# A two-layer diffusion trunk: the order of the projections, the place of the spatial gating, and pooling on GpSimd

## The chip, the cores and the metric

The kernel runs on one core of a Trainium2 chip. The metric is the device time of the whole program in microseconds (us), the median of several runs of it. Five engines work side by side, each through its own instructions in order: PE (TensorE, matmuls and transposes), DVE (VectorE), ACT (ScalarE), POOL (GpSimd) and SP (SyncE, which here only issues loads). They wait for each other on semaphores.

## The reference

A trunk of two layers on 512 latent tokens and 256 context tokens of width 1024. In each layer a modulated layer norm feeds one projection, whose columns go to four mixers; their outputs are joined, projected, and followed by a squared-ReLU network. Layer 1 keeps only what the latent tokens need: of the context it takes keys and values. Cut to the mixers:

```python
z = h @ w_in[l]                       # hc: the same for context tokens
k, v, kn, kr, vm = kv_sources(z[..., C_KV:], mla_kv_norm[l], mla_w_ukv[l])
k = apply_axial_rope(k, swa_ang_h)
q = apply_axial_rope(cols(z, C_SWA_Q, W_SWA_Q).reshape(...), swa_ang_h)
qn, qr = mla_expand_q(cols(z, C_MLA_CQ, W_MLA_CQ), mla_q_norm[l], mla_w_uq[l])
y = jnp.concatenate([
    pool_mixer(...),    # means over windows of 2, 4, 8, 16 tokens, minus the token
    swa_latent(...),    # softmax over a band of 3 blocks, the context and a sink
    mla_latent(...),    # softmax over all latent and context tokens
    sgu_mixer(...),     # u * (w_s @ layer_norm_affine(v) + b_s), with u, v = gelu(z)
], axis=-1) @ w_out[l]
```

## The kernel before, in words

Everything is float32. A matmul is made of three on parts: each operand is split into a high part (rounded by ACT) and a low part (the difference, by DVE), and high x high, high x low and low x high are added up in PSUM. So each loaded weight, and each result that goes into another matmul, passes through ACT and then DVE. The splits of loaded weights are L162 (ACT) and L165 (DVE); those of results are L145 and L146 or, with a factor, L149 and L150.

The function `mixers` computes a layer's four mixers. Its projections are called by the columns of the weight that they take:

- wb, by token: the latent queries before their norm (cq, kept in tiles cqL for latent and cqC for context tokens) and the gate's v (vgL, vgC). Its eviction `ev_b` ends with a multiply and an add by the gate norm's constants sgb (L632, L633).
- wp, by feature: the pooling mixer's input, in two tiles of features, f 0 (windows 2 and 4) and f 1 (8 and 16). Its eviction, in `pool`, copies it into a padded tile xp and makes the means by additions of shifted copies in pa and pb, and writes the difference pd.
- wk: the windowed keys. `ev_k` copies them to kf, rotates kf (a shuffle L437 and a multiply L438 on DVE, a multiply L439 on POOL, an add L440 on DVE) and splits them into kh (ACT) and kl (DVE, L654).
- wq: the windowed queries, two tiles, the same way (qf, then qs, L676).
- wu: the gate's other half u, with a gelu on ACT (L696).
- wa, by token, three groups of two token tiles: the values v, the latent keys and values before their norm (ckv) and the rotary key.

Then come the spatial gating `sgu` (a transposed weight wsT, matmuls mix, on DVE an add of bs and a multiply by u into mx, and a split into yh and yl), transposes of cq (cqT) and of ckv (ckT, krT) with their splits, and vm, the latent values. After that comes attention, in units of one query block for a pair of heads: `scores(x)`, softmax, `turn(x-1)` (the transposes pT), `values(x-2)` (the matmuls o). A table `todo` hangs other work on a unit: `rotary` (uqr, and the splits of rt and krl) on unit 1, the steps of the later heads' queries and keys on others; between them `fill` puts the ada matmuls, which make the next modulation from a streamed weight wada. In this loop the order is fixed as it is written (`self.pin`). Outside it a scheduler orders each engine's instructions by dependencies and a timeline that it plans at build; weight loads on SP's queue keep the order in which they are written.

Buffers are pools: PSUM has tiles of one bank (A, three; F, one) and of two banks (S, two, which the projections and the scores share); in SBUF the tag T, six tiles, holds xp, rc, pa, pb, kf, qf, the gate's ws, wsT and mx, p's transposes and more. A tile is handed on when its last reader is done.

## Time and profile before

| what | us |
|---|---|
| median of 3 runs (1570.26 to 1573.25) | 1571.64 |
| the profiled execution | 1570.16 |
| its span on the core | 1568.4 |
| PE busy in it | 1481.3 |
| DVE busy | 922.7 |
| ACT busy | 565.7 |
| POOL busy | 222.0 |

The profiled execution's time lies 1.8 us above its span, and 1.48 below the median of the runs. Busy times are sums over the span; they say which engine has room, not which one the end waits for. For that there is the chain that ended last, which is followed back from the last instruction. Matmuls are pipelined, so PE counts as busy also where its pace is lower; PEclk is the clock that PE was granted, as a share of the full one.

### The profile page before, as it was taken

The page shows a single profiled execution, that of the slowest core. Times are in us where ns is not written, and L with a number is a line of the kernel's source. Part 1 is how long each engine was busy: PE and PEld are TensorE (multiplying, and loading weights), DVE is VectorE, ACT ScalarE, POOL GpSimd, SP SyncE. Part 2 cuts the span into 40 slices and gives each one's busy share as a digit, 9 for nine tenths or more (in the row PEclk, how much of TensorE's full clock was granted, in tenths as well). Part 3 has the DMA queues.
Part 4 walks back from the last instruction along what each step waited for, and adds up shares of the span by engine and source line. Part 5 has one row for each costly group of instructions (what it writes and reads, how often), then busy time and mean ns, then how long its engine had stood idle before and what let it go on. Part 6 is the DMA issues. An engine that isn't in the chain of part 4 may idle for free.

```text
span 1568.4 us, 23456 instructions
## 1 busy us (share of the span) xinstructions
PE 1481.3 (94%) x9438; PEld 1246.7 (79%) x9438; DVE 922.7 (59%) x1615; ACT 565.7 (36%) x1000; POOL 222.0 (14%) x244
## 2 busy tenths in 40 slices
PE   5899889999999999999999989989998999999996
PEld 3689677787988888888888868867776888888885
DVE  4385755547545445454454798675645656655557
ACT  4433555524621221312113156355625433222322
POOL 1021334223000000000000062143222000000003
PEclk9999999999999999999999999999998999999998
DMA  8441366362232121211211223235363433333221
GB/s 296 152 120 55 112 219 195 108 242 89 81 108 65 49 76 54 76 59 55 81 55 67 81 94 111 64 109 178 120 208 108 147 95 95 95 101 92 88 81 54
DMA packets 148069, 169.93 MB, mean 108 GB/s; under 512 B 8776, under 2 KB 96248, under 8 KB 147960
## 3 DMA queue, kind: packets, MB, share of 16 engines
q1 hardware_dynamic: 137912, 149.94, 30.7%
q10 hardware_dynamic: 10048, 18.49, 3.5%
q8 instruction: 74, 1.21, 0.3%
q14 instruction: 35, 0.29, 0.1%
HBM read 164.19 MB, written 4.22 MB: 107 GB/s over the span
## 4 chain that ended last, share of the span: by engine, by line
PE 84%; DVE 7%; DMA 3%; ACT 2%; issue 1%; POOL 1%; SPq 0%; ACTq 0%; POOLq 0%; DVEq 0%
PE ff L133 54%; PE wo L133 5%; PE wb L133 3%; PE o L133 3%; PE pT L188 2%; PE wa L133 2%; PE ada L133 2%; PE wp L133 2%; PE wu L133 2%; PE wq L133 2%; PE sm L133 2%; DMA wada<-in_w_ada 1%; DVE nmax L533 1%; PE wk L133 1%; PE hT L188 1%
## 5 line engine op out<-in xcount | busy, mean ns | idle before, releaser
L162 ACT ACTIVATE hiw<-raww 128x1024 fp32r<-128x1024 f32 x120 | 126.8, 1062 | 565.8 <-PE ff L133 565.8
L165 DVE TENSOR_TENSOR low<-raww,hiw 128x1024 fp32r<-128x1024 f32 x120 | 146.3, 1223 | 245.3 <-ACT hiw L162 245.3
L133 PE MATMUL ff<-low,fh 128*128 128x512 f32 x640 | 249.0, 389 | 0.0
L133 PE MATMUL ff<-hiw,fl 128*128 128x512 f32 x640 | 249.0, 389 | 0.0
L133 PE MATMUL ff<-hiw,fh 128*128 128x512 f32 x640 | 247.9, 389 | 0.0
L133 PE MATMUL ff<-hl,hiw 128*128 128x512 f32 (+1 forms) x672 | 237.9, 354 | 0.0
L133 PE MATMUL ff<-hh,hiw 128*128 128x512 f32 (+1 forms) x672 | 237.8, 354 | 0.0
L133 PE MATMUL ff<-hh,low 128*128 128x512 f32 (+1 forms) x672 | 237.7, 354 | 0.0
L1274 DVE TENSOR_TENSOR fft<-ff,gate 128x512 f32<-128x512 f32 x160 | 110.0, 687 | 100.2 <-PE ff L133 100.2
L133 PEld LDWEIGHTS ff<-hh,hiw 128*128 128x128 f32 x672 | 127.1, 189 | 17.9
L133 PEld LDWEIGHTS ff<-hl,hiw 128*128 128x128 f32 x672 | 127.1, 189 | 17.7
L133 PEld LDWEIGHTS ff<-hh,low 128*128 128x128 f32 x672 | 127.0, 189 | 17.7
L133 PEld LDWEIGHTS ff<-hiw,fl 128*128 128x128 f32 x640 | 120.1, 188 | 25.0
L133 PEld LDWEIGHTS ff<-hiw,fh 128*128 128x128 f32 x640 | 120.2, 188 | 24.8
L133 PEld LDWEIGHTS ff<-low,fh 128*128 128x128 f32 x640 | 120.1, 188 | 24.7
L1275 POOL TENSOR_TENSOR x<-x,fft 128x512 f32<-128x512 f32 x14 | 20.3, 1452 | 837.5 <-DVE fft L1274 832.5
L547 POOL TENSOR_SCALAR p<-p,rec 128x768 f32<-128x768 f32 (+3 forms) x80 | 63.1, 793 | 142.0 <-DVE rec L546 132.1
L1275 DVE TENSOR_TENSOR x<-x,fft 128x512 f32<-128x512 f32 x114 | 78.7, 690 | 2.9
L133 PE MATMUL ada<-wada,sc 128*32 128x128 f32 x1536 | 60.7, 295 | 20.0 <-DMA wada<-in_w_ada 20.0
L133 PEld LDWEIGHTS ada<-wada,sc 128*32 128x32 f32 x1536 | 41.8, 116 | 34.1 <-DMA wada<-in_w_ada 13.1
L188 PE MATMUL pT<-ident,p 128*128 128x128 f32 x368 | 55.9, 279 | 9.9 <-ACT pT L555 4.4
L133 PE MATMUL wo<-lowo,yh 128*128 128x512 f32 x160 | 62.5, 390 | 0.5 <-DVE lowo L165 0.5
(335 smaller groups left out, 2749.7 us busy)
## 6 DMA issues: line engine op xcount, KB each, us to landing
raww<-in_w_ff SPq DMA_DIRECT2D x120, 512.0 KB, 4.2
wada<-in_w_ada SPq DMA_DIRECT2D x96, 512.0 KB, 4.6
rawwo<-in_w_out SPq DMA_DIRECT2D x16, 512.0 KB, 6.1
rawz<-in_w_ff SPq DMA_DIRECT2D x8, 512.0 KB, 5.6
rawwb<-in_w_in SPq DMA_DIRECT2D x12, 256.0 KB, 4.1
gate<-grow ACTq DMA_DIRECT2D x6, 512.0 KB, 6.8
badab<-in_b_ada SPq DMA_DIRECT2D x36, 64.0 KB, 3.9
x<-in_x SPq DMA_DIRECT2D x4, 512.0 KB, 4.4
```

The costliest lines, as they stand in the source:

```text
L133: return self.pinned(self.nc.tensor.matmul(out, lhsT, rhs, start=start, stop=stop))
L162: i = nc.scalar.activation(out=hi, in_=raw, func=AF.Copy)
L165: nc.vector.tensor_tensor(out=lo, in0=raw, in1=hi.bitcast(F32), op=ALU.subtract)
L188: return self.pinned(self.nc.tensor.transpose(out, in_, self.ident if ident is None else ident))
L533: nc.vector.tensor_reduce(out=nm, in_=S[:, lo:hi], axis=AX.X, op=ALU.max, negate=True)
L547: nc.gpsimd.tensor_scalar(out=p[:, :keep], in0=p[:, :keep], scalar1=rec, scalar2=1.0, op0=ALU.mult, op1=ALU.mult)
L1274: nc.vector.tensor_tensor(out=t, in0=ps, in1=g[:, sl], op=ALU.mult)
L1275: eng.tensor_tensor(out=xt[:, sl], in0=xt[:, sl], in1=t, op=ALU.add)
```

## The change

Five edits, which change the place and the engine of work, and none of what is computed:

1. In `ev_b`, the multiply and the add by sgb move from DVE to POOL: six token tiles in layer 0, four in layer 1, two operations of 128x256 each.
2. The transposes and splits of cq (cqT) move from behind `sgu` to right behind wb.
3. The projection wu moves from ahead of wa to behind vm, so the keys' and values' steps stand between wa and wu in the program; its weights are loaded after wa's.
4. `sgu` is called on unit 2 of the attention loop, no longer ahead of it, and its multiply by u moves from DVE to POOL.
5. In `pool`, the memsets of xp move to POOL, and so do the means of f 0; those of f 1 stay on DVE.

```diff
--- before.py
+++ after.py
@@ -629,8 +629,8 @@
             )
             m, r = self.stats(lambda _: v, 1)
             nc.vector.tensor_scalar(out=v, in0=v, scalar1=m, scalar2=r, op0=ALU.subtract, op1=ALU.mult)
-            nc.vector.tensor_tensor(out=v, in0=v, in1=P["sgb"][:, 0, :], op=ALU.mult)
-            nc.vector.tensor_tensor(out=v, in0=v, in1=P["sgb"][:, 1, :], op=ALU.add)
+            nc.gpsimd.tensor_tensor(out=v, in0=v, in1=P["sgb"][:, 0, :], op=ALU.mult)
+            nc.gpsimd.tensor_tensor(out=v, in0=v, in1=P["sgb"][:, 1, :], op=ALU.add)
 
         gb = list(zip(preps, gr))
         self.proj_tok(l, gb if full else gb[:2], [(512, 768), (1024, 1280)], 2, ev_b, "wb", self.wb_first,
@@ -639,6 +639,15 @@
         if not full:
             preps[2]()
 
+
+        cqT = [(self.Z("cqh"), self.Z("cql")) for _ in range(2)]
+        for k in range(2):
+            for s, nt, c0 in ((0, LT, 0), (1, CT, NL)) if full else ((0, LT, 0),):
+                pt = self.PA("cqT")
+                for i in range(nt):
+                    self.tr(pt[:, 128 * i:128 * i + 128], CQ[s][:, i, 128 * k:128 * k + 128])
+                n = 128 * nt
+                self.split(cqT[k][0][:, c0:c0 + n], cqT[k][1][:, c0:c0 + n], pt[:, :n], P["gq"][:, k:k + 1])
 
         pool_finish = self.pool(l, P, hL, hC, yL, yC, full)
 
@@ -688,16 +697,6 @@
                     q_split(pc, 2 * f + j, NL, NL + NC, 0.125)
 
         self.proj_T(l, hL, hC, 256, 2, ev_q, full, "wq")
-
-
-        U = [self.Z("u", F32) for _ in range(2)]
-
-        def ev_u(f, pl, pc):
-            nc.scalar.activation(out=U[f][:, :NL], in_=pl, func=AF.Gelu)
-            if full:
-                nc.scalar.activation(out=U[f][:, NL:], in_=pc, func=AF.Gelu)
-
-        self.proj_T(l, hL, hC, 768, 2, ev_u, full, "wu")
 
 
         V = self.X([128, 6, 128], "v")
@@ -736,18 +735,6 @@
 
         Wq = load_heads(A["mla_w_uq"][l].rearrange("(k p) n -> p k n", p=128), 64, 96, "uq")
         Wk = load_heads(A["mla_w_ukv"][l].rearrange("(k p) n -> p k n", p=128), 64, 128, "ukv")
-
-        self.sgu(l, P, U, VG, yL, yC, full)
-
-
-        cqT = [(self.Z("cqh"), self.Z("cql")) for _ in range(2)]
-        for k in range(2):
-            for s, nt, c0 in ((0, LT, 0), (1, CT, NL)) if full else ((0, LT, 0),):
-                pt = self.PA("cqT")
-                for i in range(nt):
-                    self.tr(pt[:, 128 * i:128 * i + 128], CQ[s][:, i, 128 * k:128 * k + 128])
-                n = 128 * nt
-                self.split(cqT[k][0][:, c0:c0 + n], cqT[k][1][:, c0:c0 + n], pt[:, :n], P["gq"][:, k:k + 1])
         ckT = (self.Z("ckh"), self.Z("ckl"))
         krf = self.T("krf", 768)
         for i0, nt, c0 in ((0, LT, 0), (LT, CT, NL)):
@@ -773,6 +760,16 @@
                 nc.vector.tensor_copy(out=dst, in_=pv[:, 0:256])
             else:
                 nc.scalar.activation(out=dst, in_=pv[:, 0:256], func=AF.Copy)
+
+
+        U = [self.Z("u", F32) for _ in range(2)]
+
+        def ev_u(f, pl, pc):
+            nc.scalar.activation(out=U[f][:, :NL], in_=pl, func=AF.Gelu)
+            if full:
+                nc.scalar.activation(out=U[f][:, NL:], in_=pc, func=AF.Gelu)
+
+        self.proj_T(l, hL, hC, 768, 2, ev_u, full, "wu")
 
 
         nq = NL + NC if full else NL
@@ -919,7 +916,7 @@
                 out_pair(O[0], NC if stream else NL, 2 + part, stream)
 
 
-        todo = {1: [rotary]}
+        todo = {1: [rotary], 2: [lambda: self.sgu(l, P, U, VG, yL, yC, full)]}
 
         def plan(part, x0, x1):
             t = part - 2
@@ -985,13 +982,13 @@
                 if ps is None:
                     continue
                 xp = self.pt.tile([128, NL + 16], F32, name=self.nm("xp"), tag="T")
-                nc.vector.memset(xp[:, 0:8], 0.0)
-                nc.vector.memset(xp[:, 8 + n:16 + n], 0.0)
+                nc.gpsimd.memset(xp[:, 0:8], 0.0)
+                nc.gpsimd.memset(xp[:, 8 + n:16 + n], 0.0)
                 x = xp[:, 8:8 + n]
                 nc.scalar.activation(out=x, in_=ps, func=AF.Copy)
                 rc = self.T("rc")
                 nc.scalar.dma_start(out=rc[:, :n], in_=A["rcnt"][f, :, c0:c0 + n])
-                tt = nc.vector.tensor_tensor
+                tt = (nc.vector if f else nc.gpsimd).tensor_tensor
                 a = self.pt.tile([128, NL + 16], F32, name=self.nm("pa"), tag="T")
                 b = self.pt.tile([128, NL + 16], F32, name=self.nm("pb"), tag="T")
                 e = 8 + n
@@ -1056,7 +1053,7 @@
                     in0=ps[:, :n].rearrange("p (c q) -> p c q", q=128),
                     in1=P["bs"][:, f, :].unsqueeze(1).to_broadcast([128, nt, 128]), op=ALU.add,
                 )
-                nc.vector.tensor_tensor(out=t[:, :n], in0=t[:, :n], in1=U[f][:, c0:c0 + n], op=ALU.mult)
+                nc.gpsimd.tensor_tensor(out=t[:, :n], in0=t[:, :n], in1=U[f][:, c0:c0 + n], op=ALU.mult)
                 if stream == 0:
                     y = (self.HL("yh"), self.HL("yl"))
                     yL[6 + f] = y
```

How the edits move instructions is seen in the order of each engine. In the rows below a row is line, operation, output<-inputs and size; x8 stands for eight alike. Rows of before have its line numbers, rows of after its own.

On PE, the end of wa in layer 0; s are the scores of unit 0. Before:

```order
L133 MATMUL wa_1540<-lowa_1403,hh_337 128x288
L133 MATMUL wa_1540<-hiwa_1402,hl_338 128x288
L188 MATMUL wsT_1625<-ident,ws_1623 128x128 x4
L133 MATMUL s_1778<-maskR,identR 128x256
L133 MATMUL s_1778<-kh_1042,qs_1124 128x256
L133 MATMUL s_1778<-kl_1044,qs_1124 128x256
L133 MATMUL s_1778<-kh_1042,qs_1124 128x256
L133 MATMUL s_1778<-kl_1044,qs_1124 128x256
L133 MATMUL mix_1632<-wsT_1630,vgL_341 64x128 x8
```

After:

```order
L133 MATMUL wa_1451<-lowa_1314,hh_337 128x288
L133 MATMUL wa_1451<-hiwa_1313,hl_338 128x288
L188 MATMUL ckT_1537<-ident,ckv_1298 128x128 x3
L188 MATMUL krT_1544<-ident,ckv_1298 96x128 x3
L133 MATMUL wu_1598<-hh_307,hiwu_1603 128x512
L133 MATMUL wu_1598<-hl_308,hiwu_1603 128x512
L133 MATMUL wu_1598<-hh_307,lowu_1604 128x512
L133 MATMUL wu_1598<-hh_309,hiwu_1603 128x512
```

The gating (wsT, mix) is gone from here, the transposes of ckv are the next thing after wa, and wu's matmuls follow.

On POOL in layer 0's projections, ahead of kf's rotation (L439); rsq and brs are roots for the norms. Before:

```order
L173 TENSOR_TENSOR rsq_832<-rv_835,mhalf 128x1
L173 TENSOR_TENSOR brs_843<-rv_844,mhalf 128x1
L173 TENSOR_TENSOR rsq_851<-rv_854,mhalf 128x1
L173 TENSOR_TENSOR brs_862<-rv_863,mhalf 128x1
L439 TENSOR_TENSOR kf_1101<-kf_1101,swa_t_869 128x512
L439 TENSOR_TENSOR qf_1239<-qf_1239,swa_t_869 128x512
```

After:

```order
L633 TENSOR_TENSOR vgC_342<-vgC_342,sgb_649 128x256
L1008 TENSOR_TENSOR pd_901<-pb_1021,xp_1014 128x512
L996 TENSOR_TENSOR pa_1033<-xp_1027 128x258
L997 TENSOR_TENSOR pb_1034<-pa_1033,rc_1031 64x256
L998 TENSOR_TENSOR pb_1034<-pa_1033 64x256
L985 MEMSET xp_1040 128x8
L986 MEMSET xp_1040 128x8
L999 TENSOR_TENSOR pb_1034<-pb_1034,rc_1031 64x256
L1008 TENSOR_TENSOR pd_901<-pb_1034,xp_1027 128x256
L985 MEMSET xp_1055 128x8
L986 MEMSET xp_1055 128x8
L439 TENSOR_TENSOR kf_1129<-kf_1129,swa_t_869 128x512
```

Gate operations (L632, L633) and the means of f 0 (L996 to L999, L1008) now stand ahead of kf's multiply.

On DVE, around unit 2 of layer 0's attention; nmax is the softmax's maximum, rec its reciprocal. Before:

```order
L591 COPY pT_1965<-pT_1972 128x128
L146 TENSOR_TENSOR rt_1921<-rt_1898,rt_1920 128x768
L146 TENSOR_TENSOR krl_1925<-krf_1718,krh_1924 32x768
L863 COPY s_2012<-sink_647 128x1
L546 RECIPROCAL rec_1961<-den_1959 128x1
L533 TENSOR_REDUCE nmax_2019<-s_2012 128x1
L863 COPY s_2027<-sink_647 128x1
L533 TENSOR_REDUCE nmax_2034<-s_2027 128x1
```

After:

```order
L591 COPY pT_1900<-pT_1907 128x128
L146 TENSOR_TENSOR rt_1856<-rt_1833,rt_1855 128x768
L146 TENSOR_TENSOR krl_1860<-krf_1536,krh_1859 32x768
L546 RECIPROCAL rec_1896<-den_1894 128x1
L1037 COPY wsT_1948<-wsT_1943 128x512
L1051 TENSOR_TENSOR mx_1959<-mix_1950,bs_652 128x512
L1051 TENSOR_TENSOR mx_1975<-mix_1966,bs_652 128x512
L146 TENSOR_TENSOR yl_1963<-mx_1959,yh_1962 128x512
L1051 TENSOR_TENSOR mx_1987<-mix_1982,bs_652 128x256
L1051 TENSOR_TENSOR mx_1999<-mix_1994,bs_652 128x256
L146 TENSOR_TENSOR yl_1979<-mx_1975,yh_1978 128x512
L860 COPY s_2012<-sink_647 128x1
```

The copy of wsT (L1037), the four adds of bs (L1051) and the splits yl (L146) stand behind krl, ahead of the next maxima.

## Rows read from the trace of the kernel before

**Rows 1.** The page's chain that ended last, over the whole span, by engine.

```profile
PE 84%; DVE 7%; DMA 3%; ACT 2%; issue 1%; POOL 1%; SPq 0%; ACTq 0%; POOLq 0%; DVEq 0%
```

**Rows 2.** The chain of layer 0's projections: start us, us, what.

```profile
107.18 16.72 PE wq L133 x96
123.90 16.70 PE wu L133 x96
...
161.86 1.28 ACT L542
...
169.03 0.66 DVE cql L150
...
186.34 0.66 PE pT L188 x6
```

**Rows 3.** Busy time by stretches: us, then busy per engine (x), PEclk, DMA share, GB/s.

```profile
96.00:140.00 44.00, 44.00 (x261) 39.14 (x260) 38.66 (x72) 18.30 (x32) 5.01 (x4) 1.00 0.31 87
159.50:186.34 26.84, 22.39 (x228) 18.27 (x227) 20.50 (x52) 13.60 (x32) 7.08 (x8) 0.94 0.36 108
172.00:175.50 3.50, 1.25 (x8) 0.79 (x8) 3.47 (x8) 2.61 (x6) 0.66 (x2) 1.00 0.57 190
175.50:179.50 4.00, 3.25 (x12) 2.69 (x12) 3.02 (x10) 0.77 (x2) 1.81 (x3) 0.57 0.03 2
957.00:993.00 36.00, 34.39 (x168) 28.13 (x166) 34.93 (x75) 19.44 (x38) 6.82 (x7) 1.00 0.40 110
1023.40:1045.36 21.96, 19.26 (x202) 15.32 (x201) 17.54 (x42) 11.65 (x27) 6.52 (x8) 1.00 0.35 120
```

**Rows 4.** PE's waits, 945 to 1024: waited for, us in total, times, longest.

```profile
PE wu L133 <- DVE kl L654: 1.2, 1, 1.2
```

**Rows 5.** The chain of layer 1's projections.

```profile
993.38 11.14 PE wu L133 x48
```

**Rows 6.** PE's timeline behind wa, layer 0: start us, us, engine line op.

```profile
179.97 0.28 PE L133 MATMUL vm<-hiukv,ckl 128*128 128x256 f32 x1
180.09 0.28 PE L133 MATMUL vm<-hiukv,ckh 128*128 128x256 f32 x1
```

**Rows 7.** DVE's timeline in layer 0, two windows; [idle before, releaser].

```profile
88.06 1.09 DVE L632 TENSOR_TENSOR vgL<-vgL,sgb 128x256 f32<-128x256 f32 x3 [2.30 <-DMA sgb<-in_sgu_norm_g]
...
109.07 0.69 DVE L1008 TENSOR_TENSOR pb<-pa 64x512 f32<-64x512 f32 x1
...
114.61 1.43 DVE L1008 TENSOR_TENSOR pb<-pa 64x256 f32<-64x256 f32 x1
...
116.79 0.42 DVE L1009 TENSOR_TENSOR pb<-pb,rc 64x256 f32<-64x256 f32 x1
...
122.83 0.87 DVE L654 TENSOR_TENSOR kl<-wk,kh 64x256 fp32r<-64x256 f32 x2
...
190.45 1.44 DVE L146 TENSOR_TENSOR krl<-krf,krh 32x768 fp32r<-32x768 f32 x1
```

**Rows 8.** POOL's timeline, layer 0's projections.

```profile
90.67 0.54 POOL L173 TENSOR_TENSOR rsq<-rv,mhalf 128x1 f32<-128x1 f32 x1 [6.57 <-DVE rv L172]
...
114.38 1.36 POOL L439 TENSOR_TENSOR kf<-kf,swa_t 128x512 f32<-128x512 f32 x1 [16.65 <-DVE rsh L437]
```

**Rows 9.** POOL's groups, whole span, by form: busy us, mean ns, idle before.

```profile
L1275 POOL TENSOR_TENSOR x<-x,fft 128x512 f32<-128x512 f32 x14 | 20.3, 1452 | 837.5 <-DVE fft L1274 832.5 <-DVE sm L347 2.5 <-DVE rv L172 2.5
...
L547 POOL TENSOR_SCALAR p<-p,rec 128x256 f32<-128x256 f32 x16 | 7.5, 478 | 19.4 <-DVE rec L546 19.1
```

**Rows 10.** ACT's timeline, layer 0's projections.

```profile
112.93 0.60 ACT L661 ACTIVATE kf<-wk 128x512 f32<-128x512 f32 x1 [4.30 <-DVE pd L1011]
```

**Rows 11.** The waits of SP's DMA queue, 150 to 330.

```profile
SPq L116 <- PE ada L133: 82.3, 23, 8.9
```

**Rows 12.** The chain in layer 0's attention.

```profile
232.68 4.35 DMA wada<-in_w_ada
...
275.00 5.21 DMA rawwo<-in_w_out
```

## The prediction, made before the changed kernel ran

> **What bounds the kernel now.** I read the page's chain first: PE holds 84% of the chain that ended last, DVE 7% [rows 1]. So what can be won is PE's idle time in the stages that the change touches, not work of the other engines. I then read the chain around the projections of both layers, the table by stretches, and the timelines of the engines behind the places where the chain leaves PE.
>
> In layer 0 PE runs wq and wu back to back, 107.18 to 140.6 [rows 2], then wa; in the stretch 96 to 140 it has no idle at all, although DVE is busy 38.66 of 44.00 us there [rows 3]. After wa the chain breaks up into pieces of other engines until the pT at 186.34 that feeds the first o [rows 2]: PE is busy 22.39 of these 26.84 us, DVE 20.50 [rows 3]. The stall is the preparation of keys, values and spatial gating, which go through DVE and ACT in turn. In the worst of it, 172 to 175.5, PE is busy 1.25 of 3.50 us, and the stretch behind that ran at a granted clock of 0.57, mostly the lower level, 1.2 of 2.4 GHz [rows 3]. Layer 1 repeats it: PE 19.26 of 21.96 us [rows 3]; there the wu before it also waits 1.2 us for DVE's kl [rows 4], in a stretch in which DVE is busy 34.93 of 36.00 [rows 3].
>
> **The change, part by part.** All sums are against the profiled execution's own time, 1570.16 us; the median of the three runs is 1571.64, that is 1.48 more, and the sum is carried over to it.
>
> *wu behind the keys and values.* wu is moved, not removed: 16.70 us in layer 0, 11.14 in layer 1 [rows 2, 5]. What stood between wa and the first o can now run under wu's matmuls. Counted from start to start in PE's timeline, at the pace of the full clock (vm 0.12 us each [rows 6]), PE's own work between 159.50 and 186.34 is about 19.0 us: wsT 0.45, mix 2.7, cqT 1.3, ckT and krT 1.6, vm 18 x 0.12 = 2.1, uqr 2.2, scores 4.8, pT 0.9, ada 2.9. Of it 4.5 (wsT, mix, cqT) leaves for another place, 14.5 stays. The rest, 26.84 - 19.0 = 7.8, is waiting and lower clock. I leave 1.0 of waiting in, because ACT has to load a table (1.28 us [rows 2]) between wu's gelu and the next exp. So the window shrinks by 26.84 - 14.5 - 1.0 = **11.3** in layer 0, by 12.3 at most. In layer 1 the same count gives 17.0 of 21.96, of which 3.1 leaves and 13.9 stays; with 0.7 of waiting left it shrinks by **7.4**, by 8.1 at most.
>
> *cqT under the projections.* 12 transposes in layer 0, 1.3 us of PE; 8 in layer 1, 0.9; and their splits on DVE, 0.66 for 512 columns [rows 2], about 2.1 in all in layer 0, in a stretch where DVE is nearly full. PE's share is in the next term.
>
> *What wu covered before.* This is the cost. In layer 0 wu starts at 123.90 [rows 2] and DVE's last kl ends at 123.70 [rows 7]: the keys are split just in time, and then wu's 16.7 us cover the queries' split. Now wa stands there. It needs the PSUM tile that wk gives back with kl, and for its third group one that is given back on DVE behind all of the qs. Two things move kl. DVE loses the pooling means of f 0 (512 columns 5 x 0.69, 256 columns 5 x 0.42 [rows 7]), two splits of wu's weights and most of the gate's operations; it gains cqT's. But kf's rotation is POOL's L439 (1.36 [rows 8]), which now stands behind 12 gate operations and 10 pooling operations on POOL's queue, and f 1's pooling on DVE needs tiles of a pool that POOL holds longer. POOL's two-tensor operation on 512 columns took 1.45 us; on 256 columns the trace has none, and I bound it by 0.48, the one-tensor operation of that width, and 0.75, half of the 512 [rows 9]. From 88.06, when the gate's constants have landed [rows 7]: 12 x 0.48 to 0.75, 5 x 1.45, 5 x 0.48 to 0.75, 6 root operations of 0.54 [rows 8], which ends between 107 and 111.5 if POOL never waits. kf came off PSUM at 112.93, after ACT had waited 4.30 for a pooling tile [rows 10]. POOL does wait, for xp from 97 on, so that wait for a tile grows rather than shrinks. The start of wa shifts against the old start of wu by 1.3 (cqT alone) to 7; I take **+4**, nearest to the row of a tile that waits. In layer 1 there is no context to pool, POOL has five such operations, and DVE sheds 8 x 0.42 + 5 x 0.69 + two weight splits (2.4) and gains 1.3 of cqT: 7.8 us less ahead of kl. The wait of 1.2 goes, 0.9 of cqT comes: **-0.3** (to +3).
>
> Two rows speak against this part: DVE's L1008 on 64x256 took 1.43 us at 114.61, inside POOL's L439, where an operation of the same size took 0.42 two microseconds later [rows 7, 8]. The Trainium skill ("SBUF — State Buffer", section "SBUF: two separate sides") has a rule that agrees: the two engines share a port pair as an exclusive lock, held for a whole instruction, against DVE operations with two SBUF inputs. By the rule moved work costs DVE part of what it saves, and the sum becomes the second rival's.
>
> *Spatial gating inside attention.* wsT and mix remain PE work: **+3.1** in layer 0, **+2.2** in layer 1. At unit 2 mix waits for DVE's copy of wsT, which stands behind nmax, pT copies, rt's and krl's L146 (krl 1.44 [rows 7]); PE's next pT stands behind mix; and the four multiplies on POOL stand ahead of later units' p. Followed in order, with every piece at its duration, PE loses 4.4 us in layer 0, at the least 1 if waits that are there anyway take the rest; I take **+3**, and **+2** (0 to 3) in layer 1.
>
> *Weight loads.* SP's loads of wada wait for PE's ada matmuls, 82.3 us in the stretch [rows 11], so they move with PE: no cost, but see the third rival.
>
> Sum: layer 0, 4 - 11.3 + 3.1 + 3 = -1.2; layer 1, -0.3 - 7.4 + 2.2 + 2 = -3.5. Together -4.7: 1565.5 for the profiled run, **1567.0** for the median. All terms at their bounds: layer 0 -6.9 to +3.2, layer 1 -6.2 to +0.8, so 1558.5 to 1575.6.
>
> **The rivals.** *Full gain.* Every cover holds: 1.3 - 12.3 + 3.1 + 1 and -0.3 - 8.1 + 2.2 + 0, together -13.1, so 1558.5. For it: DVE sheds over 7 us in each stretch where it is nearly full. Against: at unit 2 DVE's order is fixed, and wsT's copy is behind the two longest operations there.
>
> *Slower: GpSimd and DVE in each other's way.* Before kl in layer 0, DVE has some 20 operations with two SBUF inputs; one that met a POOL operation lost 1.0 us (1.43 - 0.42). If seven meet one, kl is 7 later on top of the 4, and in layer 1, if the same uses up what DVE sheds, the shift is +3 in place of -0.3. That is -4.7 + 7 + 3.3 = +5.6: 1577. It decides from 4.7 of such losses on. For it: DVE is 88 to 97% busy in both stretches. Against: POOL has 22 and 13 operations, and only those that run beside the chain to kl count.
>
> *The time is given back.* In layer 0's attention PE waits 4.35 us for wada at 232.68 and 5.21 for rawwo at 275.00 [rows 12]. If those land when they did, what layer 0 gains is waited away there, and layer 1's -3.5 shrinks to within noise with a late unit 2: -4.7 + 1.2 + 2 = -1.5, so 1570. Against it: their issue follows PE.
>
> **How the numbers follow.** About 0.2% (3.1 us) is what a measurement of this kernel can tell from no change. Forecast, -3.1 to -9: 0.42. Full gain, beyond -9: 0.12. Given back, or terms that cancel, within 3.1: 0.26. Slower: 0.20. So faster 0.54, same 0.26, slower 0.20. The range goes from the full gain, 1558.5, to the slower rival's price, 1577, and leaves about one in ten out on either side.
>
> **What would show it.** In the changed profile: from wa's end to the first o no long piece of DVE in the chain and a granted clock of 1 (window step); wa's start against 123.9 and the end of the last kl (cover step); in layer 1 no wait for kl; a wait of mix for wsT's copy, 1 to 4 us (unit-2 step); pooling operations of 1.4 us on DVE where POOL runs (lock); waits for wada and rawwo no longer than before. The prediction is wrong if wa starts after 132 in layer 0, if unit 2 costs over 5 us, or if landings hold attention where it was.

## The result, and the profile after

The changed kernel took 1581.47 us (median of four runs, 1581.25 to 1586.07); the kernel before, on the same chip, 1570.95 (four runs, 1569.59 to 1573.25). The ratio is 1.0072, with a 95% interval of 1.005 to 1.0095: slower by 0.7%. The prediction was 1567.0, in a range from 1558.5 to 1577: faster was forecast, the kernel is slower, and its time lies above the range. The profiled execution took 1581.32 us at a span of 1579.5; before it was 1570.16 at 1568.4, so 11.1 us of span are to be explained.

The page's chain of the changed kernel, by engine, against [rows 1]:

```profile
PE 78%; DVE 8%; DMA 4%; POOL 4%; ACT 3%; issue 2%; SPq 0%; ACTq 0%; POOLq 0%; DVEq 0%
```

PE gave up 6 points of the chain to everything else; POOL, which had 1%, has 4%. The table by stretches (columns as in [rows 3]) says where that is and where it isn't:

```profile
96.00:130.00 34.00, 29.84 (x194) 27.14 (x193) 24.18 (x41) 12.56 (x23) 18.83 (x24) 1.00 0.27 77
150.70:181.80 31.10, 31.10 (x260) 27.60 (x258) 14.75 (x36) 14.54 (x31) 6.96 (x8) 1.00 0.40 123
182.00:188.35 6.35, 1.94 (x49) 1.53 (x47) 5.13 (x10) 3.51 (x7) 2.94 (x3) 0.99 0.56 186
188.35:197.00 8.65, 6.30 (x52) 5.36 (x53) 4.01 (x6) 1.26 (x2) 2.54 (x2) 0.62 0.04 15
1025.10:1049.80 24.70, 24.70 (x208) 21.12 (x206) 14.59 (x36) 11.17 (x26) 6.98 (x8) 1.00 0.47 149
```

The second and the last row are the stretch from wa's end to the first o, with wu in it: PE has no idle time and the full clock, in both layers. The first row is layer 0's projections, which had no idle time before: now PE idles 4.2 of 34.0 us, and DVE, which was nearly full, is busy 24.18: it waits too. The third and fourth rows are the attention's units 1 and 2, where spatial gating now stands: PE is busy 1.94 of 6.35 us, and then comes a stretch at a granted clock of 0.62.

PE's waits from 100 to 1200 us, the stretch that the change touches (waited for: us in total, times, longest), name what is late:

```profile
PE wsT L188 <- DMA ws<-in_sgu_w: 6.4, 2, 4.4
PE wa L133 <- DVE kl L663: 6.0, 2, 4.2
...
PE sm L133 <- ACT p L542: 3.1, 1, 3.1
PE wp L133 <- DVE cqL L627: 2.7, 1, 2.7
...
PE mix L133 <- DVE wsT L1037: 1.8, 2, 0.9
PE pT L188 <- DVE mx L1051: 1.5, 1, 1.5
```

The first of them, and the longest, appears nowhere in the prediction: a wait for a DMA, the load of the spatial weights ws.

**The load of ws.** ws is loaded inside the function for spatial gating, on ACT's queue. When that function was called behind wu's evictions, the load was issued as wu began; now it goes out when the function is called, between two units. ACT's DMA issue before, then the same one after:

```profile
123.88 0.39 ACTq L1033 DMA_DIRECT2D ws<-in_sgu_w  x1
```

```profile
183.42 0.46 ACTq L1030 DMA_DIRECT2D ws<-in_sgu_w  x1
```

Before, it had 35.6 us until wsT used it at 159.50. After, PE asks for it half a microsecond later. PE's timeline behind the first o of layer 0, after:

```profile
181.84 1.09 PE L133 MATMUL o<-pT,v 128*64 128x128 f32 x16
182.86 1.08 PE L133 MATMUL ada<-wada,sc 128*32 128x128 f32 x32
188.35 1.09 PE L188 MATMUL wsT<-ident,ws 128*128 128x128 f32 x4 [4.41 <-DMA ws<-in_sgu_w]
190.31 3.68 PE L133 MATMUL mix<-wsT,vgL 128*64 128x128 f32 x32 [0.88 <-DVE wsT L1037]
193.75 1.77 PE L133 MATMUL mix<-wsT,vgC 128*64 128x128 f32 x16
197.00 0.66 PE L188 MATMUL pT<-ident,p 128*128 128x128 f32 x4 [1.48 <-DVE mx L1051]
```

PE idles 4.41 us for the load, then 0.88 for the copy of wsT; the 32 matmuls of mix take 3.68 us, where the same 32 took 1.97 before (they started at 160.88); then PE idles 1.48 until mix has been read out of PSUM. In layer 1 the load is issued at 1051 and PE waits 2.0 us.

**The keys come late.** The chain of the changed kernel in layer 0's projections, its end:

```profile
112.52 1.27 POOL pb L999
113.82 0.72 DVE pb L1002
114.56 1.13 DVE pa L1003
115.72 0.68 DVE pb L1004
116.41 0.70 DVE pb L1005
...
122.14 0.69 DVE rsh L438
...
128.61 0.42 DVE kl L663
129.05 0.44 DVE kl L663
129.62 0.50 PE wa L133 x2
```

The path runs through the means of f 0 on POOL (up to 113.8), then the means of f 1 on DVE, then the rotation of the keys, then kl, which ends at 129.49 (123.70 before, [rows 7]). wa starts at 129.62, where wu started at 123.90 [rows 2]. PE had idled 4.16 us for it, and wa's first stretch then runs at a granted clock of 0.58 (before, wa began at 1.00):

```profile
129.62:133.00 3.38, 3.38 (x16) 3.38 (x17) 3.34 (x7) 0.79 (x2) 2.21 (x2) 0.58 0.02 5
```

**What the sum became.** Stage borders read from PE's timelines of both traces (the last matmul of one stage, the first of the next):

| step | predicted, us | measured, us | from |
|---|---|---|---|
| L0, cover: wa's start against wu's old start, and wa's length | +4 | +7.7 | start +5.9 (123.7 to 129.6, PE's timeline); wa takes 21.0, not 19.2 |
| L0, window: wa's end to the first o, without wu | -11.3 | -12.8 | 27.3 to 31.2 - 16.7 |
| L0, unit 2: first o to the first pl | +6.1 (3.1 + 3) | +10.8 | 14.3 to 25.0 |
| L0, rest of attention, up to wo | 0 | +3.7 | sm to wo 69.1 to 72.8 |
| up to layer 1's wp | 0 | +1.2 | |
| L1, cover | -0.3 | +1.6 | wa's start against wu's old start is +12.2, wp's start +10.6 |
| L1, window, with wa | -7.4 | -8.3 | first o is +3.8 |
| L1, unit 2: first o to the first uq | +4.2 (2.2 + 2) | +7.7 | 16.4 to 24.1 |
| the rest | 0 | -0.5 | |
| sum | -4.7 | +11.1 | |

The two windows were right. The miss of 15.8 us lies in the two unit-2 terms (8.2 together), the two covers (5.6) and layer 0's later attention with what follows (4.9), less 2.9 from the windows and the end. In layer 0's cover (0.58 in wa's first stretch) and in both unit-2 stretches (0.86 on the whole) a lower granted clock behind a wait is part of the length.

### The profile page after: what moved, and what is told of

Read it like the earlier page. It is cut to its first block, busy times and chain, and to the rows that moved or that the text cites. A ratio compares the mean times of both kernels' runs of the same rounds, so it can differ in the third digit from the quotient of the medians.

```text
span 1579.5 us, 23437 instructions
## 1 busy us (share of the span) xinstructions
PE 1483.1 (94%) x9438; PEld 1251.4 (79%) x9438; DVE 914.2 (58%) x1562; ACT 568.6 (36%) x1002; POOL 266.9 (17%) x297
## 4 chain that ended last, share of the span: by engine, by line
PE 78%; DVE 8%; DMA 4%; POOL 4%; ACT 3%; issue 2%; SPq 0%; ACTq 0%; POOLq 0%; DVEq 0%
PE ff L133 54%; PE wo L133 4%; PE wb L133 3%; PE o L133 3%; PE wa L133 3%; PE ada L133 2%; PE pT L188 2%; PE wu L133 2%; PE sm L133 2%; DMA wada<-in_w_ada 1%; PE s L133 1%; DMA rawwo<-in_w_out 1%; DVE nmax L533 1%; PE hT L188 1%; DVE bst L180 1%
## 5 line engine op out<-in xcount | busy, mean ns | idle before, releaser
L188 PE MATMUL pT<-ident,p 128*128 128x128 f32 x368 | 56.9, 282 | 11.1 <-ACT pT L555 4.4
```

Source lines behind the costliest of these rows:

```text
L188: return self.pinned(self.nc.tensor.transpose(out, in_, self.ident if ident is None else ident))
```

## Experiments

Four suspects were to be told apart, by letters in the expectations: that ws is loaded late (theory A); that spatial gating is in the wrong place behind the first heads, whatever its load does (B); that the operations moved to GpSimd come late or get in DVE's way (C); and that the transposes of cqT, put ahead of the pooling projection wp, change the order of PE's work (D). Each ratio is to the kernel before, run on the same chip beside it, with its 95% interval. The kernel before alone took from 1570.95 to 1573.78 us (medians) on the chips used, so totals are taken from the ratios, and from traces only the lengths of stages. Stages in which nothing was edited differ by some us from kernel to kernel as well (layer 1's first uq to wo, 72.7 to 74.7 us), so a ratio alone does not tie a few us to the edited place.

**The changed kernel once more**, unedited, on another chip.

> The changed kernel itself once more, unchanged, beside the three others on the same chip. Expected: 1.007 again, and in its trace the same places: 4 to 5 us of wait for ws in layer 0 and about 2 in layer 1, some 4 of wa for kl, and a last landing of rawwo in layer 0's attention that is 2 us later, counted from the first sm, than in the kernel before. If the last is not there, it was chance of one execution.

Measured: 1.0065 (1.0048 to 1.0081), with the same waits: 6.8 us for ws (the longest 4.7), 6.4 for kl. Result and trace repeat.

**Load ws early.** The changed kernel, with ws in the unused half of the buffer for the gating's context and loaded under the projections; nothing else is changed.

```diff
-        VG = [self.G([128, 4, 256], "vgL"), self.G([128, 2, 256], "vgC") if full else None]
+        VG = [self.G([128, 4, 256], "vgL"), self.G([128, 4, 256], "vgC")]
...
+        self.ws = VG[1][:, 2:4, :].rearrange("p a b -> p (a b)")
+        nc.scalar.dma_start(
+            out=self.ws.rearrange("p (h q) -> p h q", h=4), in_=A["sgu_w"][l].rearrange("h p q -> p h q")
+        )
...
-        ws = self.T("ws")
-        nc.scalar.dma_start(
-            out=ws.rearrange("p (h q) -> p h q", h=4), in_=A["sgu_w"][l].rearrange("h p q -> p h q")
-        )
+        ws = self.ws
```

> The changed kernel with one edit: the gate's weights ws get a place of their own (the unused half of a gate tile) and are loaded under the projections, where in the changed kernel their load starts at unit 2 and PE waits 4.4 us (layer 0) and 2.0 us (layer 1) for it. Theory A (the load that moved with the gating is what the prediction left out, and the idle PE then runs mix at the lower clock): both waits are gone, mix takes 1.7 and 0.9 us again, and the time falls by 7 to 10 us, to 1571 to 1575. Theory B (the place at unit 2 costs by itself, through DVE's order): the waits for wsT's copy and for mx take over, and the time falls by less than 4 us.

Measured: 0.9999 (0.9989 to 1.0009): level with the kernel before, 10.4 to 11.5 us off the changed kernel (against its two ratios). PE's waits of this kernel:

```profile
PE wa L133 <- DVE kl L667: 6.6, 2, 4.2
...
PE pT L188 <- DVE yl L150: 3.7, 2, 2.5
PE mix L133 <- DVE wsT L1038: 3.1, 2, 1.9
PE sm L133 <- ACT p L542: 2.7, 1, 2.7
```

The wait for ws is gone, and only a part of it comes back as a longer wait for wsT's copy (3.1 in place of 1.8). From the first o to the first pl it takes 18.6 us, +4.4 on before, where the prediction had +6.1; in layer 1 +4.8, where it had +4.2. So the unit-2 step was sized about right for a gating whose load is there, and all of its miss is the load. The waits for kl come to 6.6 us, as much as before the edit, but lie elsewhere: 2.4 in layer 0 (4.2 in the changed kernel) and 4.2 in layer 1 (1.8). Of the gain, the two unit-2 stretches hold 9.3 us in these traces (25.0 to 18.6 and 24.1 to 21.2); the rest is a sum of differences in other stages (wa of layer 0 ends 3.0 us earlier, sm to wo takes 70.8 in place of 72.8, layer 1's wp to wa's end 58.8 in place of 53.6) and isn't settled.

**Spatial gating in front of attention.** The changed kernel, with the gating called behind wu and not at unit 2.

```diff
         self.proj_T(l, hL, hC, 768, 2, ev_u, full, "wu")
+        self.sgu(l, P, U, VG, yL, yC, full)
...
-        todo = {1: [rotary], 2: [lambda: self.sgu(l, P, U, VG, yL, yC, full)]}
+        todo = {1: [rotary]}
```

> The changed kernel with the gating taken out of the attention loop and called directly behind wu, everything else as changed. The load of ws then stands on ACT's queue among the evictions of wa, some 25 us ahead of its use. Theory A (late load): no wait for ws, 7 to 10 us less than the changed kernel, about as e1. Theory B (the place at unit 2): 8 to 11 us less, and at least 3 less than e1, since mix and yl then run under the first units' work.

Measured: 1.0036 (1.0024 to 1.0049), about 0.3% better than the changed kernel; the intervals just touch. The load of ws is now issued at 151.90, as wu begins, and PE never waits for it; but PE waits 8.5 us for kl (6.0 in the changed kernel). It takes the wait for ws away, as the kernel above does, and gets less for it: from wa's end to layer 0's first pl it takes 53.1 us, where the changed kernel took 56.2 and the one with ws early 49.8. The stretch from the first o to the first pl still takes 17.8 us although the gating has left it, with 3.8 us idle and a granted clock of 0.90; with the gating in it and ws there, it takes 18.6 at the full clock. So in layer 0 most of the gating's 3.1 us of PE work fills idle time at unit 2, and theory B does not hold; in layer 1 either place comes to 45.9 us from wa's end to the first uq.

**One GpSimd part back on DVE at a time, and both.** First the pooling means of f 0 with the memsets, then the gate's multiply and add, then the two edits in one kernel.

```diff
-                nc.gpsimd.memset(xp[:, 0:8], 0.0)
-                nc.gpsimd.memset(xp[:, 8 + n:16 + n], 0.0)
+                nc.vector.memset(xp[:, 0:8], 0.0)
+                nc.vector.memset(xp[:, 8 + n:16 + n], 0.0)
...
-                tt = (nc.vector if f else nc.gpsimd).tensor_tensor
+                tt = nc.vector.tensor_tensor
```

> The changed kernel with the pooling means of f 0 and the memsets back on DVE. Theory C (POOL's queue is the chain to kf: its 22 operations run from 87 to 114 us without a gap that matters): wa in layer 0 starts 3 to 5 us earlier than at 129.6, the wait of 4.2 for kl shrinks below 1, and the time falls by 3 to 6 us. Rival (DVE is full in this stretch, so the means only change the engine): wa starts within 1 us of 129.6 and the time stays within 2 us.

```diff
-            nc.gpsimd.tensor_tensor(out=v, in0=v, in1=P["sgb"][:, 0, :], op=ALU.mult)
-            nc.gpsimd.tensor_tensor(out=v, in0=v, in1=P["sgb"][:, 1, :], op=ALU.add)
+            nc.vector.tensor_tensor(out=v, in0=v, in1=P["sgb"][:, 0, :], op=ALU.mult)
+            nc.vector.tensor_tensor(out=v, in0=v, in1=P["sgb"][:, 1, :], op=ALU.add)
```

> The changed kernel with the gate norm's multiply and add back on DVE. Theory C: POOL's queue loses 12 operations (8 in layer 1), the roots for cq no longer stand behind them, so layer 1's wait of wp for cqL falls from 2.7 to about 1 us and layer 0's wa starts 2 to 4 us earlier; 3 to 6 us less. Rival: DVE, which takes the operations back, is the chain, and the time stays within 2 us.

> The changed kernel with gate and means both back on DVE, ws still loaded late and cqT still ahead of wp. Each alone gave 2 to 4 us (e3, e4). If they cost only together, this gives 8 to 11 us, ratio 0.998 to 1.001; if their cost shows only where kl sets the start of wa (with wp ahead of wk, as in e6), it gives no more than 2 to 5, ratio 1.003 to 1.005, and the two faults of the order and of GpSimd hide each other.

Measured: means back 1.0049 (1.0032 to 1.0066), gate back 1.0055 (1.004 to 1.007), both back 1.0058 (1.0036 to 1.008). Against the changed kernel's 1.0065 and 1.0072 the intervals overlap: nothing that can be told. With both back, wa of layer 0 still starts at 129.1; the first o comes 1.1 us earlier than in the changed kernel, and the first pl 0.3 later, since unit 2, with its late load, takes 26.5 us in place of 25.0. PE's waits read

```profile
PE wsT L188 <- DMA ws<-in_sgu_w: 6.9, 2, 4.8
...
PE wa L133 <- DVE kl L663: 4.3, 2, 3.1
```

By these three alone GpSimd would have been acquitted. The next ones show why that is too early: other faults hide it.

**The transposes of cqT behind the pooling projection.** The changed kernel, with these lines moved.

```diff
+        pool_finish = self.pool(l, P, hL, hC, yL, yC, full)
         cqT = [(self.Z("cqh"), self.Z("cql")) for _ in range(2)]
...
-        pool_finish = self.pool(l, P, hL, hC, yL, yC, full)
```

> The changed kernel with one edit: the transposes of cq are called behind wp, no longer ahead of it. In the changed kernel's order on PE all of wk stands ahead of three of wp's four parts, so the pooling of f 1 gets its input 5 to 7 us later than before; with this edit wp stands ahead of wk again, as before. Theory D (that order on PE, not GpSimd, delays kl): wp of layer 0 ends near 102, not 108.8, wa starts at 125 to 127, not 129.6, and the time falls by 3 to 6 us to 1575 to 1578. Theory C (POOL's queue delays kl): wa still starts at 128 to 130 and the time stays within 2 us of the changed kernel's. The wait for ws at unit 2 stays in either.

Measured: 1.0066 (1.0047 to 1.0084), no gain alone. The order does come back: in the changed kernel all of wk runs ahead of wp's two context parts (two of its four parts, not three as expected) and wp ends at 108.8; here it ends at 102.1 (101.6 before), and wa starts at 127.25. But wa then ends at 151.5, no earlier than the changed kernel's 150.7: within wa PE waits 1.9 us for DVE's rv and 0.5 for kl.

**Both: ws early and cqT behind wp.**

> The two edits together: ws loaded early (as e1) and the transposes of cq behind wp (as e5). Theories A and D together: no wait for ws, wa of layer 0 at 125 to 127, and 3 to 6 us less than e1, so a ratio to before of 0.996 to 0.998. If the ratio stays at e1's 1.000, an earlier start of attention is given back further on (at the landings of wada and rawwo).

Measured: 0.9977 (0.9967 to 0.9986), so faster than the kernel before, by 3.6 us. It has every move that the change names, only that cqT stands behind wp and not right behind wb, and its ratio is about what the prediction gave (1567.0 of 1571.64 is 0.997). That is agreement of the sum, with other terms in it (layer 0's wa still ends 5.8 us late where +4 was forecast). The first o of layer 0 comes at 179.9, where the prediction's -7.3 puts it at 179.6. PE's waits of layer 0's projections, attention and the start of layer 1 hold no ws any more, and 2.5 us for kl in place of 6.0. What keeps it from more is the next series.

**wsT transposed under the projections** as well, on top of the last one: the transposes and their copy are moved directly behind wq, so that at unit 2 only mix and what follows it are left. `sgu` then takes the finished tile.

```diff
+        pt = self.PA("wsT")
+        for h in range(4):
+            self.tr(pt[:, 128 * h:128 * h + 128], self.ws[:, 128 * h:128 * h + 128])
+        nc.vector.tensor_copy(out=self.ws, in_=pt)
...
+        wT = ws
```

> As e6, and ws is also transposed under the projections, behind wq, so that at unit 2 only mix and what follows it are left. In e1 mix waited 3.1 us for wsT's copy in the two layers (1.9 at most). If the placement at unit 2 costs through DVE's order, this takes 2 to 4 us off e6: ratio 0.993 to 0.997. If what is lost there is given back later anyway, the ratio is e6's within 0.001.

Measured: 0.9983 (0.9974 to 0.9992): nothing, where 2 to 4 us less had been held possible. First o to first pl stays at 18.5. The wait for wsT's copy is gone (3.1 us with ws early), and others stand in its place: 2.0 us of mix for mx, and 4.5 in place of 3.7 of pT for yl.

**No means and no gate on GpSimd**, on top of ws early and cqT behind wp: the two DVE edits above, added to that kernel. The multiply by u stays on GpSimd.

> As e6 (ws loaded early, cqT behind wp), and both the gate norm's operations and the means of f 0 back on DVE, so that only the multiply by u is left on GpSimd. If the moves to GpSimd help where DVE is full, kl comes later than in e6 (wa of layer 0 starts after 128) and the ratio rises to 1.000 to 1.003. If they hurt (POOL's queue, the two engines in each other's way), wa starts before 126 and the ratio falls to 0.993 to 0.996. Within 0.0015 of e6: they are an exchange without effect.

Measured: 0.9913 (0.9899 to 0.9928), 1560.07 us against 1573.13. It has the lowest ratio of all, 0.9% ahead of the kernel before and some 24 us ahead of the changed one on the same chip (1583.74 in the repeat above). Its table by stretches, and PE at unit 2:

```profile
96.00:130.00 34.00, 34.00 (x219) 30.99 (x218) 33.21 (x66) 14.24 (x26) 5.02 (x4) 1.00 0.27 75
145.20:176.30 31.10, 31.10 (x260) 27.60 (x258) 14.75 (x36) 14.53 (x31) 6.79 (x8) 1.00 0.41 126
```

```profile
178.41 0.66 PE L188 MATMUL wsT<-ident,vgC 128*128 128x128 f32 x4
180.96 1.97 PE L133 MATMUL mix<-wsT,vgL 128*64 128x128 f32 x32 [1.89 <-DVE wsT L1038]
```

PE's idle time in the projections is gone with POOL's work there (5.02 us in place of 18.83), although DVE is busy 33.21 of 34.00: more DVE work, and no wait for it. Here the transposes of ws wait for nothing, and mix, after 1.89 us of wait for their copy, takes 1.97 us again. wa starts at 125.0, 20.0 us pass from wq's end to wa's end (25.2 in the changed kernel, 22.5 in the one that this builds on), and no wait of PE for kl is left.

**One GpSimd part added to that fastest kernel at a time**: the gate, the means; and the multiply by u taken off GpSimd, so that nothing of the change is on it.

> e9 (ws early, cqT behind wp, gate and means on DVE; ratio 0.991) with the gate norm's operations on GpSimd, as the change had them. If they are what costs (roots and cq's scaling wait behind them on POOL, and DVE is held up beside them), the ratio is within 0.002 of e6's, 0.998; if the means are, it stays near 0.991 to 0.993.

> e9 with the means of f 0 and the memsets on GpSimd, as the change had them, and the gate on DVE. If the means are what costs (kf's rotation behind ten operations of 1.3 us), the ratio is 0.996 to 0.998; if not, 0.991 to 0.993. If neither e13 nor e14 comes near 0.998, only both together cost, because POOL's queue is then long enough to reach kf.

```diff
-                nc.gpsimd.tensor_tensor(out=t[:, :n], in0=t[:, :n], in1=U[f][:, c0:c0 + n], op=ALU.mult)
+                nc.vector.tensor_tensor(out=t[:, :n], in0=t[:, :n], in1=U[f][:, c0:c0 + n], op=ALU.mult)
```

> e9 with the multiply by u on DVE as well, so that nothing is moved to GpSimd. The multiply took 1.28 us on POOL for 512 columns, against 0.69 on DVE, and stands in the chain of unit 2; if that chain sets the time there, 1 to 3 us less, ratio 0.989 to 0.991; if DVE's order at unit 2 does, 0.991 to 0.993.

Measured: gate on GpSimd 0.993 (0.9915 to 0.9945), means on GpSimd 0.9965 (0.9951 to 0.9979), multiply on DVE 0.9959 (0.9943 to 0.9975). So the means cost 8.2 us (their interval stands clear of the fastest one's), the gate 2.7 (the intervals overlap), and putting the multiply back on DVE costs 7.2, which had not been expected. The kernel with the means on GpSimd, in the stretch of the projections:

```profile
96.00:130.00 34.00, 32.36 (x209) 29.41 (x208) 30.05 (x45) 13.15 (x24) 16.05 (x19) 1.00 0.27 72
```

PE idles 1.64 us there again, all of it waiting for kl, and POOL is busy 16.05; in layer 1 PE waits 2.1 us for kl. In the kernel with the multiply on DVE, PE's waits from 940 to 1075 begin with two that the fastest one lacks, though in the place of the first the fastest one has a wait of 2.5 us, for yl:

```profile
PE pT L188 <- POOL mkh L808: 3.0, 1, 3.0
PE wa L133 <- DVE kl L667: 2.0, 1, 2.0
```

Only some 2 us of its loss stand at the multiply's own place (layer 1, first o to first uq, 21.6 in place of 19.6); 2.7 more are in layer 0 from sm to wo and 2.0 in layer 1's wait for kl, where nothing was edited. How the one leads to the other is open, and so is whether the multiply's engine itself is worth more than those 2 us.

**Only wu moved.** The kernel before, with wu behind the keys and values and the gating directly behind wu, all operations on the engines that they had.

```diff
-        self.proj_T(l, hL, hC, 768, 2, ev_u, full, "wu")
...
-        self.sgu(l, P, U, VG, yL, yC, full)
...
+        self.proj_T(l, hL, hC, 768, 2, ev_u, full, "wu")
+        self.sgu(l, P, U, VG, yL, yC, full)
```

> The kernel before with one edit of the five: wu is moved behind vm, and the gating, which needs it, directly behind wu, ahead of attention; cqT stays behind wa, every operation on its engine of before. The window step alone: if keys and values are hidden under wu at no cost, the first o comes 6 to 9 us earlier in either layer less the gating's own stall (3 to 5 us), so 1563 to 1569, ratio 0.995 to 0.998. If the cover that wu gave the keys is worth as much, or the gating's chain simply stands where keys and values stood, the ratio is 0.999 to 1.003.

Measured: 0.9949 (0.9934 to 0.9964): one edit of the change, alone, is worth 8 us. wa starts at 124.0, right where wu had started: the cover that wu gave was not needed. From wa's end to the first o, without wu, it takes 20.4 us in place of 27.3, with the gating still in it. This is the window step by itself. Part of it is given back behind the first o of layer 0: the stretch to the first pl takes 17.3 us in place of 14.3, at a granted clock of 0.90, though the gating is not in it.

**The same, with the gating at unit 2** and ws loaded early; then with the gating at unit 2 in layer 0 alone.

```diff
-        todo = {1: [rotary]}
+        todo = {1: [rotary], 2: [lambda: self.sgu(l, P, U, VG, yL, yC, full)]}
```

> e7 (before with wu behind vm alone, ratio 0.995), with the gating moved to unit 2 and ws loaded early; cqT, gate, means and multiply stay as before. In e6 the gating cost 4.8 us between first o and uq in layer 1, where e7, with the gating ahead of attention, paid 2.5 in the stretch ahead; in layer 0 e6 was 6.0 better ahead of the first o and 1.3 worse behind it. So layer 0 gains 3 to 5 against e7 and layer 1 loses 2 to 3: ratio 0.992 to 0.996. If the place at unit 2 is bad in both layers: 0.997 to 1.000.

```diff
+        todo = {1: [rotary]}
+        if full:
+            todo[2] = [lambda: self.sgu(l, P, U, VG, yL, yC, full)]
```

> As e10, but the gating at unit 2 in layer 0 only, ahead of attention in layer 1. If the reading of the two layers is right, it keeps layer 0's 3 to 5 us and avoids layer 1's loss: ratio 0.990 to 0.994, the best of all. If the gain of layer 0 is given back at the landings in its attention, the ratio is e7's, 0.995.

Measured: 0.9955 (0.9941 to 0.997) and 0.9935 (0.992 to 0.995), against 0.9949: the three intervals overlap. With everything on DVE, the gating's place is worth nothing that can be measured. In the traces two effects cancel: with the gating at unit 2, wa's end to the first pl takes 51.2 us in place of 54.4 in layer 0, but wa's end to the first uq 47.3 in place of 43.6 in layer 1. The fastest kernel's interval stands clear of 0.9949 and 0.9955, and overlaps that of 0.9935. From the kernel of 0.9955 it differs in the place of cqT and in the multiply by u on GpSimd; with that multiply back on DVE it was level with it (0.9959).

## Why the prediction was wrong, by its own steps

**Unit 2: the step that failed.** The prediction followed wsT's copy, mx and p through DVE's and POOL's queues, and said that mix would wait 1 to 4 us for the copy (it waits 0.9). It took ws as loaded. The function that was moved issues that load itself, and where the prediction weighs weight loads it speaks of SP's queue alone; the one on ACT's it never asked about. That term, +6.1 and +4.2, came out as +10.8 and +7.7; with the load in time it is +4.4 and +4.8. Taking that wait away gave 10.4 to 11.5 us back, 9.3 of them in these two stretches of the traces. This is shown. The prediction named a cost of over 5 us at unit 2 as a sign that it is wrong; beyond the gating's 3.1 us of PE work it cost 7.7. The wait has a price beyond its 4.41 us: PE had been busy 1.94 of 6.35 us, and the granted clock of the next stretch was 0.62, mostly the lower of its two levels, 1.2 of 2.4 GHz; mix took 3.68 us in place of 1.97.

**The covers: one mechanism was named and half right, the size was low, and a second cause was missed.** The sum counted POOL's operations in front of kf and took +4; the same points moved by 7.7 in layer 0, 5.9 in wa's start and 1.8 in its length, most of that from the granted clock of 0.58. In layer 1 they moved by +1.6, not -0.3; the wait of 1.2 for kl, which was to go, became 1.8. kf's rotation on POOL did not stand behind POOL's queue: POOL had been idle for 5.13 us when it began (its row stands below, under the rivals). What POOL held up is f 1's pooling on DVE, ahead of kf, as the prediction also said, and by more than tiles: its first mean waits for POOL's memset of xp, its second for POOL's last mean of f 0:

```profile
112.48 0.71 DVE L1001 TENSOR_TENSOR pa<-xp 128x526 f32<-128x526 f32 x1 [1.50 <-POOL xp L986]
113.82 0.70 DVE L1002 TENSOR_TENSOR pb<-pa 128x524 f32<-128x524 f32 x1 [0.64 <-POOL pb L999]
```

The bounds for a two-tensor operation of 256 columns on POOL, 0.48 to 0.75 us, held for 11 of the 12 gate operations of layer 0, but not for the five of the context's means, which took 0.61 to 1.43 us, 5.8 together in place of 2.4 to 3.75. POOL's pooling ended at 115.1; the count had it end by 111.5 if POOL never waits. POOL's timeline of the changed kernel, layer 0 and, last, layer 1:

```profile
87.22 2.13 POOL L632 TENSOR_TENSOR vgL<-vgL,sgb 128x256 f32<-128x256 f32 x3 [2.76 <-DMA sgb<-in_sgu_norm_g]
...
104.81 1.67 POOL L633 TENSOR_TENSOR vgC<-vgC,sgb 128x256 f32<-128x256 f32 x1
...
965.37 3.12 POOL L632 TENSOR_TENSOR vgL<-vgL,sgb 128x256 f32<-128x256 f32 x1 [1.50 <-DVE vgL L631]
...
969.33 1.53 POOL L173 TENSOR_TENSOR rsq<-rv,mhalf 128x1 f32<-128x1 f32 x1
```

In layer 1 the gate's multiply of 3.12 us and its add stand ahead of the root that cq waits for, on POOL's queue: rsq ends at 970.9, and PE's wp waits 2.7 us for cqL (0.8 before). The prediction had listed the roots among POOL's operations, and not that they have to queue behind the gate. The second cause is the order on PE: with cqT ahead of wp, wp ends 7.2 us later (108.8, not 101.6), and with it f 1's pooling: ACT copies its input at 109.53 in place of 102.63, and its first mean on DVE starts at 112.48 in place of 104.81, the memset above included. The prediction costed cqT at its 1.3 us of PE. Undone alone it gave nothing; undone together with the load it gave a further 3.5 us (0.9999 to 0.9977).

**The window: right.** -12.8 and -8.3 for -11.3 and -7.4, no wait and a full clock from wa's end to the first o; the 1.0 and 0.7 us of waiting that the sum had left in did not come. The kernel with only wu moved, 8 us faster, shows the step alone.

**Layer 0's later attention: not foreseen.** The prediction feared that landings would hold attention where it was, and priced that as layer 0's gain lost, not as a stage that grows. sm to wo became 3.7 us longer. ACT's timeline there, before and then after (the four splits of w_out and the p behind them):

```profile
280.29 1.06 ACT L162 ACTIVATE hiwo<-rawwo 128x1024 fp32r<-128x1024 f32 x1 [2.10 <-DMA rawwo<-in_w_out]
...
284.95 1.05 ACT L162 ACTIVATE hiwo<-rawwo 128x1024 fp32r<-128x1024 f32 x1
285.91 0.90 ACT L542 ACTIVATE p<-sm,nmax 128x768 f32<-128x768 f32 x1
```

```profile
284.49 1.06 ACT L162 ACTIVATE hiwo<-rawwo 128x1024 fp32r<-128x1024 f32 x1 [0.62 <-DMA rawwo<-in_w_out]
...
292.56 1.06 ACT L162 ACTIVATE hiwo<-rawwo 128x1024 fp32r<-128x1024 f32 x1 [2.64 <-DMA rawwo<-in_w_out]
293.53 0.88 ACT L542 ACTIVATE p<-sm,nmax 128x768 f32<-128x768 f32 x1
```

Counted from the first sm (242.4 and 248.1), the first split is 1.5 us earlier and the fourth 1.9 later, because its load lands later; p stands behind it on ACT, and PE waits 3.1 us for p. The same stage took 68.2 to 73.4 us across the kernels tried, whatever was edited in front of it. What sets the landing is open, and so are these 3.7 us.

**The rivals.** "GpSimd and DVE in each other's way" was priced at 10.3 us (7 + 3.3) over the forecast. Taking the means and the gate off GpSimd, once load and order were mended, was worth 0.0064 of the time, 10 us. So the size came near its price, which is luck as far as is known, since seven meetings were not shown; and it is not what made this kernel slow: with both taken off the changed kernel the time did not move by what can be measured, kl still ended late by PE's order, and unit 2 took back what the first o had gained. How much of the 10 us is operations that meet, and how much the wait of f 1's pooling and of cq for POOL's queue, wasn't separated. For meeting speak two places of the changed kernel. In layer 0 DVE's 64x256 operation, begun while POOL rotated kf, took 1.43 us, as the same size had before [rows 7, 8], and ended 0.3 us after POOL's; POOL's row, then DVE's:

```profile
120.46 1.37 POOL L439 TENSOR_TENSOR kf<-kf,swa_t 128x512 f32<-128x512 f32 x1 [5.13 <-DVE rsh L437]
```

```profile
120.68 1.43 DVE L1005 TENSOR_TENSOR pb<-pa 64x256 f32<-64x256 f32 x1
```

And POOL's 3.12 us of layer 1, above, fell on three DVE operations with two SBUF inputs, two of them weight splits, and ended 0.6 us after the last:

```profile
965.21 1.22 DVE L165 TENSOR_TENSOR lowp<-rawwp,hiwp 128x1024 fp32r<-128x1024 f32 x1
966.35 0.41 DVE L388 TENSOR_TENSOR hl<-hfull,hh 128x256 fp32r<-128x256 f32 x1
966.68 1.21 DVE L165 TENSOR_TENSOR lowp<-rawwp,hiwp 128x1024 fp32r<-128x1024 f32 x1
```

The Trainium skill ("SBUF — State Buffer", section "SBUF: two separate sides") has an exclusive lock between the two, held for a whole instruction, against DVE operations with two SBUF inputs; both places agree with it, though in the second POOL stayed out across three of them in a row. "The time is given back" did not happen as described: the windows' gain was there at the first o, and lost at unit 2; from the first pl to the first sm, where wada lands, both kernels took 41.2 us.

## What to carry to other kernels

When a function is moved, list every instruction in it that isn't arithmetic first: the load that it issues moves too, and loses the lead that its old place gave it; hoist it to where it was. When several edits are made at once and undoing one of them gives nothing, undo it again on top of the mended ones: here the means cost nothing measurable in the changed kernel and 8 us in the mended one. An engine with idle time is no free place for work on the way to the next stage: the means, which the keys wait for, cost 8 us on GpSimd, though it was busy for only 222.0 of 1568.4 us before. The multiply by u came out ahead there; that this is so because it stands at the end of a chain is not shown.

## What the runs showed that had not been expected

A wait of 4.41 us inside attention cost a further 1.7 us in the matmuls behind it (3.68 for 1.97), through the granted clock of 0.62, and one of 4.16 us ahead of wa the same way (0.58 for the next 3.38 us). One two-tensor operation of 128x256 on GpSimd took from 0.73 to 3.12 us in the same kernel, so a duration from a stretch where DVE stands still is no price for one where it runs. The multiply by u, in layer 0 four operations of 4.34 us together on GpSimd in the fastest kernel, came out 7.2 us ahead of the same kernel with it on DVE, though DVE does each in 0.41 to 0.69; only some 2 of the 7.2 stand at its place.
